# Routing with the dot-product row in PSUM, all four look-up scalings on ScalarE, and more rows fetched

## The chip, the cores and the metric

The kernel runs on one core of a Trainium2 chip (trn2). The metric is the device time of one execution, in microseconds (us); the time given is the median of several runs. Times inside an execution come from one profiled execution of the same program.

## The reference, cut to what matters

The reference is two transformer blocks over 512 tokens of 1024 features. Only the end of the second block is touched: a mixture of 16384 single-row experts (PEER), chosen by product keys.

```python
def peer_ffn(u, w_q, sub_keys, u_tab, v_tab):        # u: 512 tokens x 1024
    q = (xt @ w_q).reshape(T, H, 2, PEER_DKEY // 2)   # 8 heads, 2 halves
    s = jnp.einsum('thcd,hcnd->thcn', q, sub_keys)    # 128 keys a half
    top_s, top_i = lax.top_k(s, K)                    # K = 16
    cand = top_s[:, :, 0, :, None] + top_s[:, :, 1, None, :]
    best_s, best_j = lax.top_k(cand.reshape(T, H, K * K), K)
    expert = ...                                      # i * 128 + j of the 16 best pairs
    g = jax.nn.softmax(best_s, axis=-1)
    act = gelu(einsum('cd,chkd->chk', xc, u_tab[expert]))
    return einsum('chk,chkd->cd', g * act, v_tab[expert])
```

The last step of all is an RMS norm of the residual plus this sum.

## The kernel before, in words

The kernel computes the experts in two ways. For the first 128 tokens it **fetches** the chosen rows: 128 steps gather one row of `u_tab` for each token (GpSimd, indirect DMA, 512 KB, `grow`, 7 buffers) and take the dot product with the token's row `xr` on VectorE (L1252), and 128 more gather rows of `v_tab` and add them up (L1263). Each of the two runs has six steps of lag, so there are 268 steps in all (`self.left`, L1210). For the other 384 tokens it computes **all** experts densely: 128 blocks, each of 24 matmuls over 384 columns (`mm<-ushi,whi` and its kin, L136 to L138), a Gelu (L119) and later three products with the rows of `v_tab` for each of three token blocks (L1567). The gate of each expert and token is made by **look-up matrices**: for four tokens at a time `onehots` (L1420) compares a row of numbers (`iota`, in the PSUM tile `tables`) with the chosen indices, which gives J and I, and multiplies I by the token's weights; four matmuls J x I (L1449) then write a group `pg` into PSUM, and ScalarE copies it to `stg` (L1450), from where it goes to memory (`Gd`). There are 96 such groups, 32 for each of three token blocks.

In `onehots` the compare is one VectorE instruction (L1423). ScalarE then scales `NA` = 2 of the four I matrices (L1427) and VectorE the other two (L1428), with a copy `wp` of the weights in `tables`.

The order of the stage is set in `route`. First a loop over 16 score blocks (L1300 to L1325): a projection of 24 matmuls over 512 columns, four score matmuls into a PSUM tile `psc` (L1312), `topk` on VectorE; in its first eight rounds two transposes give a part of `xr` and of `gacc` (L1321 to L1325). The `tr` tile that they pass through has one buffer. Then, under `manual_schedule` for the PE, one dense block after another is issued (L1473 to L1483), and behind each so many steps of `routing()` as the block's credit pays for: `choose` (VectorE work that picks the experts of one token block) and `gates` (onehots three groups ahead, `AHEAD`, and the group's four matmuls). A block earns `UCOST` = 2.9 (4.04 before the fetching begins), a group costs `GCOST` = 0.7, a step of `choose` 1 to 6.6. The PE executes in exactly this order. The other engines' orders are laid out by the framework's planner, which takes, for each engine, the earliest issued instruction among those that it holds for ready; each engine executes its queue in order.

After each block `fetch_steps(RATE * (256 - e))` (L1483) adds to a credit `left / units` fetch steps. By the costs in the source 61 blocks are issued in this loop and 45 of the 268 fetch steps.

PSUM has eight banks: two for `mm`, four for `psc` and `pg` together (one tag), one for `tr`, one for `tables`. At the end of `route` its six banks are given back, and `combine` takes them as six accumulators `acc`, which first receive transposes of the residual (L1573). `combine` then runs the remaining blocks, the products with `v_tab` and the remaining fetch steps.

Of the kernel before, what the change touches and what calls it, by code (L numbers as in the profile page):

```python
# [7 lines left out]
F32 = mybir.dt.float32  # L8
# [26 lines left out]
FLEAD = 4  # L35
LAST = 3
GCOST = 0.7
NA = 2
UCOST = 2.9
AHEAD = 3  # L40
RATE = 1.3


class Stream:
# [51 lines left out]
class Kernel:  # L96
# [1133 lines left out]
    def gathered(self, ep):  # L1230
# [15 lines left out]
        for k in range(P + lag):  # L1246
            if k < P:
                rows[k] = fetch(a["peer_ur_2"], k)
            if k >= lag:
                scr = ep.tile([P, D], BF16, name="gscr", tag="gscr", bufs=1)  # L1250
                with after():
                    nc.vector.scalar_tensor_tensor(scr, rows.pop(k - lag), 1.0, self.xr, op0=ALU.mult,  # L1252
                                                   op1=ALU.mult, accum_out=self.gact[:, k - lag:k - lag + 1])
            if k == P + lag - 1:
                self.act(self.gact, self.gact, AF.Gelu)
                nc.vector.tensor_tensor(self.gw, self.gw, self.gact, op=ALU.mult)
            yield
# [19 lines left out]
    def route(self, ep, rp, pp):  # L1277
        tc, nc, a = self.tc, self.nc, self.a
        sk = rp.tile([P, 16, P], F32, name="sk", tag="cand")
        nc.sync.dma_start(sk, a["peer_sk"])  # L1280

        iota_s = rp.tile([P, P], F32, name="iota", tag="tables")
        nc.gpsimd.iota(iota_s, pattern=[[1, P]], base=0, channel_multiplier=0, allow_small_or_imprecise_dtypes=True)
        tables = pp.tile([P, 3 * P + 16], F32, name="tables", tag="tables", bufs=1)
        iota, first = tables[:, :P], tables[:, 3 * P:]
        nc.vector.tensor_copy(iota, iota_s)
        tv = rp.tile([P, 4, 16, 16], F32, name="tv")
        tix = rp.tile([P, 4, 16, 16], U32, name="tix")
# [11 lines left out]
        for b in range(16):  # L1300
# [6 lines left out]
            qt = rp.tile([P, 2, S], F32, name="pq", tag="oh", bufs=AHEAD + 1)  # L1307
            q = qt[:, 0]
            nc.vector.tensor_tensor(q, ps, self.rstd, op=ALU.mult)
            pc = pp.tile([P, 4, P], F32, name="psc", tag="psc", bufs=4)  # L1310
            for tb in range(4):
                nc.tensor.matmul(pc[:, tb, :], q[:, tb * P:(tb + 1) * P], sk[:, b, :], start=True, stop=True)  # L1312
            for tb in range(4):
# [1 line left out]
            if b < 8:  # L1315
                t = qt[:, 1]
                nc.vector.scalar_tensor_tensor(t, self.xT[:, b, :], self.g["norm_ffn_2"][:, b:b + 1], self.rstd,
                                               op0=ALU.mult, op1=ALU.mult)
                self.split(self.us[0][:, b, :], self.us[1][:, b, :], t[:, P:])
                px = pp.tile([P, 2, P], F32, name="tr", tag="tr", bufs=1)  # L1320
                nc.tensor.transpose(px[:, 0], t[:, :P], self.ident)  # L1321
                nc.tensor.transpose(px[:, 1], self.xT[:, b, :P], self.ident)
                bs = slice(b * P, (b + 1) * P)
                nc.scalar.activation(self.xr[:, bs], px[:, 0], AF.Copy)
                nc.scalar.activation(self.gacc[:, bs], px[:, 1], AF.Copy)  # L1325


# [21 lines left out]
        def choose(tb):  # L1349
# [62 lines left out]
                nc.tensor.transpose(pt[:, c, :], ijw[:, c].rearrange("p h k -> p (h k)"), self.ident)  # L1412
            t = rp.tile([P, 3, P], F32, name="ijwT", tag="ijwT", bufs=2)
            nc.vector.tensor_copy(t, pt[:, :3])
            wp = tables[:, (1 + tb % 2) * P:(2 + tb % 2) * P]
            nc.vector.tensor_copy(wp, t[:, 2])
            T[tb] = t, wp
            yield 1.0

        def onehots(t, wp, x0):  # L1420

            oh = rp.tile([P, 2, 4, P], F32, name="oh", tag="oh", bufs=AHEAD + 1)
            nc.vector.tensor_tensor(oh, iota[:, None, None, :].to_broadcast([P, 2, 4, P]),  # L1423
                                    t[:, 0:2, x0:x0 + 4, None].to_broadcast([P, 2, 4, P]), op=ALU.is_equal)
            I, J = oh[:, 0], oh[:, 1]
            for c in range(NA):
                nc.scalar.activation(I[:, c], I[:, c], AF.Copy, scale=t[:, 2, x0 + c:x0 + c + 1])  # L1427
            self.last_gate = nc.vector.tensor_tensor(I[:, NA:], I[:, NA:], wp[:, x0 + NA:x0 + 4, None]  # L1428
                                                     .to_broadcast([P, 4 - NA, P]), op=ALU.mult)
            return J, I  # L1430

        def gates(tb):

            t, wp = T.pop(tb)
            oh = {}
            for x in range(0, 4 * AHEAD, 4):
                oh[x] = onehots(t, wp, x)
                yield 1.2
            for part in range(4):
                self.write(len(self.pieces) - P // PIECE)  # L1440
                stg = self.cp.tile([P, P, 32], F32, name="stg", tag="xlo" if part % 2 else "xhi")
                for k in range(8):
                    x = 32 * part + 4 * k
                    if x + 4 * AHEAD < P:
                        oh[x + 4 * AHEAD] = onehots(t, wp, x + 4 * AHEAD)
                    J, I = oh.pop(x)
                    pg = pp.tile([P, 4, P], F32, name="pg", tag="psc", bufs=4)
                    for c in range(4):
                        nc.tensor.matmul(pg[:, c, :], J[:, c], I[:, c], start=True, stop=True)  # L1449
                    nc.scalar.activation(stg[:, :, 4 * k:4 * k + 4], pg.rearrange("p c i -> p i c"), AF.Copy)  # L1450
                    yield GCOST
# [45 lines left out]
    def combine(self, ep, e):  # L1497
        tc, nc, a = self.tc, self.nc, self.a
        with tc.tile_pool(name="pv", bufs=1) as vp, tc.tile_pool(name="pvp", bufs=1, space=PSUM) as pp:
            self.ws.all_vector = True  # L1500
            ng = vp.tile([P, D], F32, name="ng")
            nc.gpsimd.dma_start(ng, a["norm_final_2"].to_broadcast([P, D]))
            vh = self.cp.tile([P, 4, D], F32R, name="vh", tag="xhi")
# [206 lines left out]
```

## Time and profile before

| | us |
|---|---|
| median of 3 runs | 2456.24 (2454.66 to 2459.8) |
| profiled execution, its own time | 2457.38 |
| span of the profiled execution, first to last instruction | 2455.7 |
| score stage of the routing (16 projections) | about 1173 to 1276 |
| choosing for the first two token blocks | 1276 to 1357 |
| gates, first two token blocks, with choosing between | 1357 to 1555 |
| gates, third token block | 1555 to 1628 |
| change to `combine` | 1628 to 1672 |
| `combine` | 1672 to 2448 |

In the views, PE is TensorE's matmuls, PEld its weight loads, DVE is VectorE, ACT ScalarE, POOL GpSimd. A form such as `oh<-tables,ijwT` names the tile written and the tiles read. Matmuls are pipelined and their recorded durations overlap, so the pace of a run of matmuls is read from starts, not from durations. Each matmul record of L1449 is one of two that a 128x128 product in fp32 leaves, so a group has eight.

### The profile page before, as it was taken

To read this page: it belongs to the slowest core of one execution; us is meant where nothing else is said; L and a number is where in the kernel's file an instruction comes from. 1 tells how busy PE (TensorE), PEld (TensorE's weight loads), DVE (VectorE), ACT (ScalarE), POOL (GpSimd) and SP (SyncE) were. 2 spreads that over 40 slices of the span, in tenths; PEclk is the share of its full clock that TensorE was granted. 3 is DMA by queue.
4 is the path that set the end of the run, shared out by engine and by line. 5 is a ranking of instruction groups with operands and counts; after the bars stand their busy time and mean duration, and the time that the engine had idled before them with its cause. 6 is when DMAs were issued, how large, how long until landed. Compare 5 with 4: busy or idle time off the path is not lost.

```text
span 2455.7 us, 32561 instructions
## 1 busy us (share of the span) xinstructions
PE 2388.6 (97%) x11857; PEld 2019.8 (82%) x11857; DVE 1765.5 (72%) x3088; ACT 1085.1 (44%) x1847; POOL 981.5 (40%) x564
## 2 busy tenths in 40 slices
PE   8999999999999999999999999989999999999998
PEld 6776788888776767887789999989888888888887
DVE  7986777721567564365999998967887678777884
ACT  5565332322466575434323656653333333333333
POOL 5332444444542313542336556533343234434430
PEclk9999999999999999999999999999999999999999
DMA  4111233333322202231236687889999889998981
GB/s 139 61 60 44 95 94 96 99 89 96 114 93 73 86 27 69 95 107 65 78 97 221 217 293 265 296 325 354 322 344 343 287 289 343 340 322 310 339 305 69
DMA packets 178673, 451.96 MB, mean 184 GB/s; under 512 B 16480, under 2 KB 83200, under 8 KB 175312
## 3 DMA queue, kind: packets, MB, share of 16 engines
q1 hardware_dynamic: 129616, 299.07, 36.1%
q0 software_dynamic: 37232, 135.07, 15.1%
q10 hardware_dynamic: 11664, 15.74, 1.8%
q8 instruction: 93, 1.52, 0.3%
q14 instruction: 68, 0.56, 0.1%
HBM read 409.98 MB, written 39.85 MB: 183 GB/s over the span
## 4 chain that ended last, share of the span: by engine, by line
PE 78%; DVE 15%; ACT 3%; issue 2%; POOL 1%; DMA 1%; ACTq 0%; SPq 0%; DVEq 0%; POOLq 0%
PE acc L1567 21%; PE mm L136 15%; PE mm L137 15%; PE mm L138 15%; PE pg L1449 3%; DVE cv L375 1%; DVE oh L1423 1%; PE av L1007 1%; PE tr L661 1%; DVE gscr L1252 1%; POOL wlo L74 1%; DMA vraw<-in_peer_v 1%; DVE xlo L172 1%; PE sc L637 1%; ACT whi L70 1%
## 5 line engine op out<-in xcount | busy, mean ns | idle before, releaser
L74 POOL TENSOR_TENSOR wlo<-wraw,whi 128x1024 fp32r<-128x1024 f32 (+1 forms) x250 | 602.5, 2412 | 825.0 <-ACT whi L70 761.9
L70 ACT ACTIVATE whi<-wraw 128x1024 fp32r<-128x1024 f32 (+1 forms) x319 | 334.4, 1049 | 608.5 <-PE mm L137 412.2
L136 PE MATMUL mm<-xhi,whi 128*128 128x512 f32 x952 | 383.5, 403 | 4.7 <-DVE gb L403 2.1
L138 PE MATMUL mm<-xhi,wlo 128*128 128x512 f32 x952 | 377.7, 397 | 1.3 <-POOL wlo L74 1.2
L137 PE MATMUL mm<-xlo,whi 128*128 128x512 f32 x952 | 377.4, 396 | 0.0
L136 PE MATMUL mm<-ushi,whi 128*128 128x384 f32 x1024 | 349.5, 341 | 9.5 <-ACT act L119 9.5
L138 PE MATMUL mm<-ushi,wlo 128*128 128x384 f32 x1024 | 346.0, 338 | 0.0
L137 PE MATMUL mm<-uslo,whi 128*128 128x384 f32 x1024 | 345.8, 338 | 0.0
L1567 PE MATMUL acc<-vh,galo 128*128 128x512 f32 x768 | 300.3, 391 | 0.0
L1567 PE MATMUL acc<-vl,gahi 128*128 128x512 f32 x768 | 300.2, 391 | 0.0
L1567 PE MATMUL acc<-vh,gahi 128*128 128x512 f32 x768 | 299.0, 389 | 0.0
L1238 POOL DMA_INDIRECT grow<-in_peer_v,gidx x128 | 184.7, 1443 | 269.8 <-DVE gacc L1263 254.5
L1238 POOL DMA_INDIRECT grow<-in_peer_ur,gidx x128 | 152.5, 1191 | 248.8 <-DVE gscr L1252 228.9
L136 PEld LDWEIGHTS mm<-xhi,whi 128*128 128x128 f32 x952 | 180.2, 189 | 46.9 <-issue 9.4
L137 PEld LDWEIGHTS mm<-xlo,whi 128*128 128x128 f32 x952 | 179.5, 189 | 40.8 <-issue 4.5
L138 PEld LDWEIGHTS mm<-xhi,wlo 128*128 128x128 f32 x952 | 179.9, 189 | 39.3 <-POOL wlo L74 1.9
L193 ACT ACTIVATE gahi<-gg 128x384 fp32r<-128x384 f32 x128 | 67.3, 526 | 319.4 <-PE acc L1567 245.2
L136 PEld LDWEIGHTS mm<-ushi,whi 128*128 128x128 f32 x1024 | 194.8, 190 | 12.6 <-ACT act L119 10.2
L137 PEld LDWEIGHTS mm<-uslo,whi 128*128 128x128 f32 x1024 | 194.5, 190 | 2.4
L138 PEld LDWEIGHTS mm<-ushi,wlo 128*128 128x128 f32 x1024 | 194.3, 190 | 0.0
L72 DVE TENSOR_TENSOR wlo<-wraw,whi 128x1024 fp32r<-128x1024 f32 x69 | 85.8, 1244 | 137.8 <-ACT whi L70 137.7
L1252 DVE SCALAR_TENSOR_TENSOR gscr<-grow,xr 128x1024 bf16<-128x1024 f32 x128 | 176.3, 1377 | 0.5
(438 smaller groups left out, 4433.1 us busy)
## 6 DMA issues: line engine op xcount, KB each, us to landing
wraw<-in_peer_u SPq DMA_DIRECT2D x128, 512.0 KB, 4.5
vraw<-in_peer_v SPq DMA_DIRECT2D x128, 512.0 KB, 6.9
Gd<-stg SPq DMA_DIRECT2D x24, 1024.0 KB, 8.9
rgat<-Gd SPq DMA_DIRECT2D x32, 768.0 KB, 9.7
wraw<-in_w_up SPq DMA_DIRECT2D x44, 512.0 KB, 3.5
Ad<-act ACTq DMA_DIRECT2D x64, 192.0 KB, 4.0
ract<-Ad SPq DMA_DIRECT2D x64, 192.0 KB, 7.5
wraw<-in_w_in SPq DMA_DIRECT2D x20, 512.0 KB, 3.5
```

The source lines that it names most:

```text
L70: self.nc.scalar.activation(hi[:, :w], raw[:, :w], AF.Copy)
L72: self.nc.vector.tensor_tensor(lo[:, :w], raw[:, :w], hi[:, :w].bitcast(F32), op=ALU.subtract)
L74: self.last_split = self.nc.gpsimd.tensor_tensor(lo[:, :w], raw[:, :w], hi[:, :w].bitcast(F32), op=ALU.subtract)
L136: mm(ps, w[0], x[0], start=start, stop=False)
L137: mm(ps, w[0], x[1], start=False, stop=False)
L138: mm(ps, w[1], x[0], start=False, stop=stop)
L172: nc.vector.scalar_tensor_tensor(lo[:, db, :n], xb, g[:, db:db + 1], hi[:, db, :n].bitcast(F32), op0=ALU.mult, op1=ALU.subtract)
L193: self.nc.scalar.activation(hi, src, AF.Copy)
L1238: nc.gpsimd.indirect_dma_start(out=t, out_offset=None, in_=tab.rearrange("a b d -> (a b) d"), in_offset=bass.IndirectOffsetOnAxis(ap=self. ...
L1252: nc.vector.scalar_tensor_tensor(scr, rows.pop(k - lag), 1.0, self.xr, op0=ALU.mult, op1=ALU.mult, accum_out=self.gact[:, k - lag:k - lag ...
L1449: nc.tensor.matmul(pg[:, c, :], J[:, c], I[:, c], start=True, stop=True)
L1567: mm(acc[tb][h], x[:, ts], v[:, i % 4, ds], start=False, stop=(i == P - 1 and x is lo), skip_group_check=True)
```

## The change

- `xps`, a PSUM tile of 128x1024 fp32 (two banks), takes in the first eight score rounds a copy of what `xr` takes, by one VectorE copy of 128x128 a round. While the routing runs, the dot products of the fetched rows read `xps` instead of `xr`; from `combine` on they read `xr` again.
- `onehots` loses VectorE's multiplication: ScalarE scales all four I matrices. `wp` and its copy are gone, and `tables` shrinks within its bank.
- `psc` and `pg` have two buffers together instead of four, which frees the two banks for `xps`.
- `RATE` goes from 1.3 to 1.05: by the source 55 instead of 45 fetch steps are issued in the routing loop. The number of blocks, the groups behind each and the costs stay as they are.

```diff
-NA = 2
-RATE = 1.3
+RATE = 1.05
...
+                x = self.xr if self.xps is None else self.xps
...
-                    nc.vector.scalar_tensor_tensor(scr, rows.pop(k - lag), 1.0, self.xr, op0=ALU.mult,
+                    nc.vector.scalar_tensor_tensor(scr, rows.pop(k - lag), 1.0, x, op0=ALU.mult,
...
+        self.xps = pp.tile([P, D], F32, name="xps")
...
-        tables = pp.tile([P, 3 * P + 16], F32, name="tables", tag="tables", bufs=1)
-        iota, first = tables[:, :P], tables[:, 3 * P:]
+        tables = pp.tile([P, P + 16], F32, name="tables", tag="tables", bufs=1)
+        iota, first = tables[:, :P], tables[:, P:]
...
-            pc = pp.tile([P, 4, P], F32, name="psc", tag="psc", bufs=4)
+            pc = pp.tile([P, 4, P], F32, name="psc", tag="psc", bufs=2)
...
                 nc.scalar.activation(self.xr[:, bs], px[:, 0], AF.Copy)
+                nc.vector.tensor_copy(self.xps[:, bs], px[:, 0])
...
-            wp = tables[:, (1 + tb % 2) * P:(2 + tb % 2) * P]
-            nc.vector.tensor_copy(wp, t[:, 2])
-            T[tb] = t, wp
+            T[tb] = t
...
-            nc.vector.tensor_tensor(oh, iota[:, None, None, :].to_broadcast([P, 2, 4, P]),
+            self.last_gate = nc.vector.tensor_tensor(oh, iota[:, None, None, :].to_broadcast([P, 2, 4, P]),
                                     t[:, 0:2, x0:x0 + 4, None].to_broadcast([P, 2, 4, P]), op=ALU.is_equal)
             I, J = oh[:, 0], oh[:, 1]
-            for c in range(NA):
+            for c in range(4):
                 nc.scalar.activation(I[:, c], I[:, c], AF.Copy, scale=t[:, 2, x0 + c:x0 + c + 1])
-            self.last_gate = nc.vector.tensor_tensor(I[:, NA:], I[:, NA:], wp[:, x0 + NA:x0 + 4, None]
-                                                     .to_broadcast([P, 4 - NA, P]), op=ALU.mult)
...
-                    pg = pp.tile([P, 4, P], F32, name="pg", tag="psc", bufs=4)
+                    pg = pp.tile([P, 4, P], F32, name="pg", tag="psc", bufs=2)
...
+            self.xps = None
```

## Rows read from the trace of the kernel before

**Rows 1.** The page, part 1: busy time, share of the span, instructions.

```profile
PE 2388.6 (97%) x11857; PEld 2019.8 (82%) x11857; DVE 1765.5 (72%) x3088; ACT 1085.1 (44%) x1847; POOL 981.5 (40%) x564
```

**Rows 2.** Busy time by stretch; columns in the first line.

```profile
core 0: us, PE busy (x) PEld busy (x) DVE busy (x) ACT busy (x) POOL busy (x), PEclk, DMA share, GB/s
1173.00:1276.00 103.00, 102.48 (x515) 83.42 (x514) 99.82 (x533) 22.15 (x40) 35.70 (x15) 1.00 0.25 79
1276.00:1357.40 81.40, 74.43 (x412) 73.34 (x410) 80.47 (x288) 30.76 (x43) 45.53 (x24) 0.96 0.58 192
1357.40:1555.00 197.60, 194.92 (x1283) 194.28 (x1284) 186.58 (x277) 123.05 (x255) 115.43 (x63) 0.99 0.77 270
1555.00:1628.40 73.40, 73.40 (x526) 73.23 (x524) 68.52 (x93) 53.20 (x124) 35.01 (x22) 1.00 0.81 290
1672.00:2448.00 776.00, 776.00 (x3748) 683.99 (x3747) 593.65 (x748) 276.76 (x391) 281.98 (x205) 1.00 0.86 306
```

**Rows 3.** PE's waits from 1165 to 1680: total us, times, longest us.

```profile
PE mm L136 <- ACT act L119: 9.5, 2, 6.3
PE tr L1412 <- DVE ijw L1345: 2.1, 1, 2.1
PE tr L1412 <- DVE tmp L1344: 1.6, 1, 1.6
PE pg L1449 <- ACT oh L1427: 1.4, 2, 1.0
PE pg L1449 <- DVE oh L1428: 1.3, 1, 1.3
PE acc L1573 <- ACT stg L1450: 1.0, 1, 1.0
```

**Rows 4.** Groups of instructions, 1354 to 1630: count | busy us, mean ns | idle before, releaser.

```profile
L1423 DVE TENSOR_TENSOR oh<-tables,ijwT 128x1024 f32<-128x1024 f32 x96 | 116.9, 1218 | 8.4 <-ACT whi L70 3.9 <-PE pg L1449 3.7
...
L1252 DVE SCALAR_TENSOR_TENSOR gscr<-grow,xr 128x1024 bf16<-128x1024 f32 x42 | 71.3, 1698 | 0.2
...
L1427 ACT ACTIVATE oh<-oh,ijwT 128x128 f32<-128x128 f32 x192 | 68.0, 396 | 70.7 <-DVE oh L1423 68.9
...
L1238 POOL DMA_INDIRECT grow<-in_peer_ur,gidx x41 | 45.6, 1111 | 50.1 <-DVE gscr L1252 37.3 <-PE mm L138 7.1 <-issue 2.0
L1428 DVE TENSOR_TENSOR oh<-oh,tables 128x256 f32<-128x256 f32 x96 | 40.1, 417 | 2.5
```

**Rows 5.** The same view in `combine`, 1700 to 1945, where POOL runs no arithmetic.

```profile
L1252 DVE SCALAR_TENSOR_TENSOR gscr<-grow,xr 128x1024 bf16<-128x1024 f32 x72 | 87.9, 1220 | 0.2
```

**Rows 6.** Timeline of ACT in a block with four groups: start, us, instruction, wait before.

```profile
1604.25 1.06 ACT L70 ACTIVATE whi<-wraw 128x1024 fp32r<-128x1024 f32 x1 [1.04 <-issue]
1605.21 0.47 ACT L119 ACTIVATE act<-mm 128x384 f32<-128x384 f32 x1
1605.58 0.39 ACT L1427 ACTIVATE oh<-oh,ijwT 128x128 f32<-128x128 f32 x1
...
1606.39 0.58 ACT L1450 ACTIVATE stg<-pg 128x512 f32<-128x512 f32 x1
1606.87 0.68 ACT L1427 ACTIVATE oh<-oh,ijwT 128x128 f32<-128x128 f32 x2
1607.46 1.07 ACT L1450 ACTIVATE stg<-pg 128x512 f32<-128x512 f32 x2
```

**Rows 7.** Timeline of PE, runs of groups of L1449 (eight records a group).

```profile
1539.58 2.84 PE L1449 MATMUL pg<-oh 128*128 128x128 f32 x24
...
1604.17 3.73 PE L1449 MATMUL pg<-oh 128*128 128x128 f32 x32
1611.91 3.73 PE L1449 MATMUL pg<-oh 128*128 128x128 f32 x32
```

**Rows 8.** Timeline of ACT, the first copy behind the run of three groups of rows 7.

```profile
1540.98 0.59 ACT L1450 ACTIVATE stg<-pg 128x512 f32<-128x512 f32 x1
```

**Rows 9.** Timeline of DVE: a copy of 128x128 into PSUM.

```profile
1423.11 0.28 DVE L1401 COPY tr<-ixf 128x128 f32<-128x128 f32 x1
```

More of the change, by code (lines that the diff above doesn't have):

```diff
@@ L1414, in choose, with onehots @@
             nc.vector.tensor_copy(t, pt[:, :3])
-            wp = tables[:, (1 + tb % 2) * P:(2 + tb % 2) * P]
-            nc.vector.tensor_copy(wp, t[:, 2])
-            T[tb] = t, wp
+            T[tb] = t
             yield 1.0
-        def onehots(t, wp, x0):
+        def onehots(t, x0):
             oh = rp.tile([P, 2, 4, P], F32, name="oh", tag="oh", bufs=AHEAD + 1)
-            nc.vector.tensor_tensor(oh, iota[:, None, None, :].to_broadcast([P, 2, 4, P]),
+            self.last_gate = nc.vector.tensor_tensor(oh, iota[:, None, None, :].to_broadcast([P, 2, 4, P]),
                                     t[:, 0:2, x0:x0 + 4, None].to_broadcast([P, 2, 4, P]), op=ALU.is_equal)
             I, J = oh[:, 0], oh[:, 1]
-            for c in range(NA):
+            for c in range(4):
                 nc.scalar.activation(I[:, c], I[:, c], AF.Copy, scale=t[:, 2, x0 + c:x0 + c + 1])
-            self.last_gate = nc.vector.tensor_tensor(I[:, NA:], I[:, NA:], wp[:, x0 + NA:x0 + 4, None]
-                                                     .to_broadcast([P, 4 - NA, P]), op=ALU.mult)
             return J, I
         def gates(tb):
-            t, wp = T.pop(tb)
+            t = T.pop(tb)
             oh = {}
             for x in range(0, 4 * AHEAD, 4):
-                oh[x] = onehots(t, wp, x)
+                oh[x] = onehots(t, x)
                 yield 1.2
@@ L1444, in gates @@
                     if x + 4 * AHEAD < P:
-                        oh[x + 4 * AHEAD] = onehots(t, wp, x + 4 * AHEAD)
+                        oh[x + 4 * AHEAD] = onehots(t, x + 4 * AHEAD)
                     J, I = oh.pop(x)
-                    pg = pp.tile([P, 4, P], F32, name="pg", tag="psc", bufs=4)
+                    pg = pp.tile([P, 4, P], F32, name="pg", tag="psc", bufs=2)
                     for c in range(4):
```

## The prediction

> **What bounds the kernel now.** I read the busy times first: TensorE is at 97% of the span [rows 1]. An average can hide a stage with another limit, so the stretches come next [rows 2]. In `combine` the PE is busy in all of 776 us, and no wait of it is recorded there: nothing that the change moves into or out of `combine` can shorten it. In the routing, 1276 to 1628, the reader sees two engines near their limit at once: the PE at 74.43 of 81.4, 194.92 of 197.6 and 73.4 of 73.4 us, VectorE at 80.47, 186.58 and 68.52. VectorE looks like the bound, but it is so only where the PE waits, and the waits of the PE [rows 3] are short: 3.7 us at L1412 and 3.2 of the 9.5 us at L136, both before the first gate, while VectorE chooses the experts of the second token block; 1.4 + 1.3 = 2.7 us behind onehots; then, at the change to `combine`, 1.0 us for the last copy and 6.3 us for a Gelu. That is 17.2 us in all. The PE's order and its work stay as they are, so this sum is the ceiling of any gain, and only the 2.7 us hang on what the change relieves.
>
> **VectorE's relief.** The removed multiplications are 96 x 0.417 = 40.1 us [rows 4]. The dot products took 1.698 us in the routing and 1.220 us in `combine`, where POOL runs no arithmetic [rows 4, 5]. The compare of onehots has as many elements and one operand in PSUM, and took 1.218 us under the same POOL [rows 4]. So I take 1.22 us for a dot product with `xps`, 42 x 0.478 = 20.1 us less; the bounds are 1.70 and 1.22. [...] Ten more fetch steps add 10 x 1.3 = 13 us. VectorE's load from 1357 to 1628 falls from 255 to 255 - 40 - 20 + 13 = 208 of 271 us. What that is worth is the wait behind it: 2.7 us, bounds 0 and 2.7. The 6.9 us before the first gate stay: in that stretch there is no dot product and no onehot yet.
>
> **The copies into `xps`.** Eight copies of 128x128, 0.28 us each [rows 9], go to VectorE in the score stage, 2.2 us. VectorE has 3.2 us idle there and the PE 0.5 [rows 2], so the PE paces the stage and VectorE's gaps take the copies; I count 0. If that cover is gone they lengthen the later wait at L1412 by up to 2.2 us. The copy is queued on VectorE ahead of `topk`, and `tr` (one buffer) is not free before it is done; the next transposes come a round later.
>
> **Ten fetch steps moved.** Each is a descriptor instruction on POOL, a 512 KB transfer and a dot product. POOL: 10 x 1.1 us [rows 4] beside 150 of 271 us busy [rows 2]; queued behind it is the weights' low half (`wlo`), of which two blocks are in stock. The DMA engines are at 0.77 to 0.81 [rows 2]; 5 MB in 271 us are 19 GB/s beside 270 to 290. Cost 0, bounds 0 and some 3 us at the change to `combine`, where the transfers collide with those of `vraw`. `acc` now takes over the banks of `xps` and so waits for the last dot product of the routing; one or two of them may still run then, 0 to 2.4 us [rows 5]. In `combine` ten steps less gain nothing, for the PE was never idle there.
>
> **ScalarE and the two buffers.** This is the term that counts. Two scalings in a row start 0.59 us before the next copy (1606.87 to 1607.46, [rows 6]). Two more for each of 96 groups are 96 x 0.59 = 57 us. Between 1555 and 1628 ScalarE goes from 53.2 to 53.2 + 32 x 0.59 = 72 of 73.4 us: it becomes as full as the PE. In 1357 to 1555 it goes from 123 to 161 of 197.6. [...]
>
> Now the buffers. A group takes the PE 3.73 - 2.84 = 0.89 us, and a block with four groups comes every 7.74 us [rows 7]. With four buffers a run of four groups waits for nobody. With two, the third group waits for the copy of the first, the fourth for that of the second. Take the run at 1604.17 [rows 7]: the third group would start at 1604.17 + 1.78 = 1605.95, but ScalarE first works through the split of weights, the Gelu and two scalings, and ends the first copy at 1606.39 + 0.58 = 1606.97 [rows 6]: 1.02 us late. The third group then ends at 1607.86, the second copy at about 1608.0: another 0.15. So 1.2 us for a run of four with ScalarE's queue as it was. If two more scalings stand ahead of each copy, the first copy comes 1.6 us late and the second another 0.75: 2.35 us. If the copy stands ahead of the scalings, as in the run of three at 1539.58 (third group due at 1541.36, first copy done at 1540.98 + 0.59 = 1541.57, [rows 7, 8]), it is 0.2 us. For a run of four there is a floor all the same: ScalarE's own sequence, 5.8 us in rows 6 (0.96 + 0.37 + 0.2 for the queued store, and four times 0.59 + 0.48), becomes 8.2 us in a block of 7.74: 0.45 us.
>
> By the source's credits 9 blocks have four groups or five, 12 have three. Low: 9 x 0.45 + 12 x 0 = 4. High: 9 x 2.35 + 12 x 1.6 = 40. I take 1.2 for fours, in the middle, since VectorE, now early, lets ScalarE do some scalings while the dense block runs but also lets the planner put others ahead of a copy; and 0.3 for threes, near the row of 1539, because ScalarE has slack there: 9 x 1.2 + 12 x 0.3 = 14.4.
>
> **Sum.** 14.4 - 2.7 = +11.7 us on the profiled execution's 2457.4: 2469.1. That execution stands 1.1 us above the median of the runs, so 2468.
>
> **Rivals.** (a) *Copies first.* The planner lays the copies ahead of the scalings nearly everywhere, and VectorE's waits vanish: 9 x 0.45 + 12 x 0.2 - 2.7 = +3.8, so 2460: not slower by what can be told. For it: the orders at 1539 [rows 8]; against it: the run at 1604 [rows 6], and in a block's issue order the scalings of the group three ahead stand before the copy. (b) *Scalings first everywhere*: 40 us and no gain, 2457.4 - 1.1 + 37 to 40, some 2495. It decides once 1.2 us of scalings stand between the Gelu and the first copy of a block. (c) *Faster at the change to `combine`*, one mechanism: the 6.3 us Gelu there [rows 3] is queued behind other work of ScalarE. If the new order puts it ahead, 6.3 us go, and with 2.7 us of onehot waits and the floor of 3 to 4 us the kernel takes 2456.2 - 6.3 - 2.7 + 3.5 = 2451 or a little less. Against it: nothing of the change touches that place but the banks and the fetches, and these rather add. (d) *The PSUM operand does not speed the dot products*: then VectorE stands at 228 of 271 us, still below its old 255, and the time is as in the forecast.
>
> **How the numbers follow.** Forecast (2462 to 2476, d included) 0.46; b and what leads to it, above 2476, 0.16; a, 2452 to 2461, 0.27; c, below 2451, 0.11. A measurement of this kernel can tell about 0.2%, 4.9 us, from no change, so faster than 2451.3 counts as faster and slower than 2461.1 as slower: 0.11, 0.27, 0.62. The range leaves out the far part of b and of c: 2450 to 2487.
>
> **What would show it.** In the profile of the changed kernel: no L1428; L1252 at about 1.22 us in the routing; VectorE near 77% from 1357 on; four scalings a group and ScalarE above 90% in the last token block's gates; waits of the PE's `pg` matmuls for ScalarE (`stg`), most at the third and fourth group of a run, some 14 us together; blocks with four groups 8.2 to 10 us apart instead of 7.74; `combine` at its 776 us. I am wrong if the PE's waits for `stg` are below 5 us, if the pace of these blocks stays at 7.74, or if the score stage, with two buffers now, stretches.

## The result, and the profile after

| | before | after |
|---|---|---|
| median (7 runs each) | 2456.24 us | 2469.07 us |
| lowest and highest | 2452.47 to 2459.8 | 2464.66 to 2472.25 |
| profiled execution, span | 2457.38, 2455.7 | 2469.26, 2467.5 |

The ratio of after to before is 1.0052, with a 95% interval of 1.0039 to 1.0065: 9.6 to 16.0 us slower. The forecast was 2468. The total agrees, but the terms of the sum do not, and most of what follows is about that.

Part 1 of the page of the changed kernel, to lay beside [rows 1]:

```profile
PE 2390.6 (97%) x11857; PEld 2018.4 (82%) x11857; DVE 1711.0 (69%) x2997; ACT 1143.4 (46%) x2039; POOL 970.6 (39%) x564
```

TensorE has the same instructions and the same share. VectorE is 54 us lighter and ScalarE 58 us heavier; nothing in this line tells that the kernel became slower. The stretches do, in the view that answers to [rows 2]; each of the first four stretches begins and ends at nearly the same work as there, and the last two are cut at the first product in `acc`, at 1684.90 (columns as in [rows 2]):

```profile
1173.00:1276.00 103.00, 102.56 (x522) 84.82 (x522) 100.84 (x549) 25.21 (x41) 36.25 (x16) 1.00 0.25 82
1276.00:1359.80 83.80, 72.44 (x402) 71.32 (x401) 82.83 (x278) 30.18 (x46) 46.60 (x25) 0.95 0.58 195
1359.80:1558.00 198.20, 195.64 (x1266) 193.60 (x1267) 152.35 (x229) 157.56 (x374) 114.47 (x69) 0.99 0.79 283
1558.00:1647.60 89.60, 80.19 (x542) 76.81 (x540) 57.06 (x65) 73.82 (x192) 38.52 (x25) 1.00 0.75 266
1647.60:1684.90 37.30, 34.99 (x218) 34.62 (x218) 17.17 (x19) 14.99 (x22) 1.83 (x3) 1.00 1.02 378
1684.90:2460.00 775.10, 775.10 (x3742) 682.88 (x3741) 582.89 (x728) 276.88 (x390) 268.70 (x196) 1.00 0.85 301
```

The gates of the third token block take 89.6 us where they took 73.4, and the PE, busy in all of it before, is idle for 9.4 us. The score stage (103 us) and `combine` have kept their length (from the first product in `acc` to the last 775.7 us before and 775.6 after). There are two smaller differences: the stretch before the first gate is 2.4 us longer, and the change to `combine` is shorter. The PE's waits from 1160 to 1700 (us, times, longest) answer to [rows 3]:

```profile
PE pg L1447 <- ACT stg L1448: 10.3, 11, 1.5
PE mm L135 <- ACT act L118: 6.8, 2, 5.5
PE tr L1414 <- DVE tmp L1346: 2.9, 1, 2.9
PE tr L1414 <- DVE ijw L1347: 2.1, 1, 2.1
PE acc L1572 <- ACT stg L1448: 1.0, 1, 1.0
PE tr L1414 <- DVE ijw L1380: 0.9, 1, 0.9
```

The waits for onehots are gone, a new wait of the `pg` matmuls for the copies to `stg` has come, and the Gelu waits have changed places: 5.5 us now stand before the first gate (3.2 in [rows 3]) and 1.3 us at the change to `combine` (6.3 there).

For all kernels below I cut the routing at three marks. The **way** runs from the first score matmul to the first matmul after the PE's Gelu wait ahead of the first gate; the **gates** from there to the first transpose into `acc`; the **change** from there to the first product in `acc`. These lengths are differences of start times in the timeline of the PE of one profiled execution each; a ratio is taken to runs of the kernel before on the same chip, so that rows are better compared by ratios than by medians:

| kernel | way | gates | change | median us | ratio to before |
|---|---|---|---|---|---|
| before | 183.2 | 272.0 | 43.6 | 2456.24 | |
| after | 186.0 | 288.8 | 36.2 | 2469.07 | 1.0052 [1.0039, 1.0065] |
| e1_two_buffers | 183.2 | 293.6 | 40.3 | 2476.66 | 1.0087 [1.0073, 1.0100] |
| e2_four_scalings | 183.6 | 269.8 | 43.4 | 2454.02 | 0.9997 [0.9988, 1.0006] |
| e3_rate | 186.7 | 279.2 | 42.4 | 2463.14 | 1.0036 [1.0023, 1.0050] |
| e4_copies_first | 186.0 | 277.4 | 42.4 | 2462.57 | 1.0030 [1.0018, 1.0041] |
| e8_old_rate | 182.4 | 289.2 | 38.2 | 2467.90 | 1.0058 [1.0045, 1.0072] |
| e9_psum_row_only | 182.0 | 285.8 | 40.9 | 2464.93 | 1.0042 [1.0028, 1.0056] |
| e10_gelu_first | 183.6 | 269.9 | 42.7 | 2453.66 | 0.9996 [0.9987, 1.0005] |
| e11_no_fetch | 183.6 | 269.8 | 34.7 | 2445.16 | 0.9957 [0.9943, 0.9971] |
| e12_both | 183.6 | 269.9 | 34.6 | 2446.15 | 0.9965 [0.9953, 0.9977] |
| e13_after_no_fetch | 186.0 | 288.8 | 34.6 | 2466.46 | 1.0043 [1.0029, 1.0057] |

From before to after the three stretches change by +2.8, +16.8 and -7.4: +12.2 us (the spans differ by 11.8; the median by 12.8).

### The profile page after: what moved, and what is told of

Same layout as the page of the kernel before. It is cut to its first block, busy times and chain, and to the rows that moved or that the text cites. A ratio compares the mean times of both kernels' runs of the same rounds, so it can differ in the third digit from the quotient of the medians.

```text
span 2467.5 us, 32759 instructions
## 1 busy us (share of the span) xinstructions
PE 2390.6 (97%) x11857; PEld 2018.4 (82%) x11857; DVE 1711.0 (69%) x2997; ACT 1143.4 (46%) x2039; POOL 970.6 (39%) x564
## 3 DMA queue, kind: packets, MB, share of 16 engines
q1 hardware_dynamic: 129616, 299.07, 36.2%
## 4 chain that ended last, share of the span: by engine, by line
PE 79%; DVE 12%; ACT 5%; issue 2%; DMA 1%; POOL 1%; DVEq 0%; SPq 0%; POOLq 0%; ACTq 0%
PE acc L1566 21%; PE mm L135 16%; PE mm L136 16%; PE mm L137 15%; PE pg L1447 2%; DVE cv L374 1%; ACT oh L1427 1%; PE av L1006 1%; ACT whi L69 1%; PE tr L660 1%; POOL wlo L73 1%; DVE xlo L171 1%; PE sc L636 1%; PE psc L1313 1%; PE sc L637 0%
## 5 line engine op out<-in xcount | busy, mean ns | idle before, releaser
L1237 POOL DMA_INDIRECT grow<-in_peer_ur,gidx x128 | 146.8, 1147 | 219.0 <-DVE gscr L1252 195.9
L136 PEld LDWEIGHTS mm<-xlo,whi 128*128 128x128 f32 x952 | 179.6, 189 | 40.9 <-issue 4.5
L1566 PEld LDWEIGHTS acc<-vh,galo 128*128 128x128 f32 x768 | 144.1, 188 | 30.1
```

The costliest lines, as they stand in the source:

```text
L136: mm(ps, w[0], x[1], start=False, stop=False)
L1237: nc.gpsimd.indirect_dma_start(out=t, out_offset=None, in_=tab.rearrange("a b d -> (a b) d"), in_offset=bass.IndirectOffsetOnAxis(ap=self. ...
L1566: mm(acc[tb][h], x[:, ts], v[:, i % 4, ds], start=False, stop=(i == P - 1 and x is lo), skip_group_check=True)
```

## The experiments

**Each part alone.** Three kernels take one part of the change each onto the kernel before.

Two buffers for `psc` and `pg`, nothing else:

```diff
-            pc = pp.tile([P, 4, P], F32, name="psc", tag="psc", bufs=4)
+            pc = pp.tile([P, 4, P], F32, name="psc", tag="psc", bufs=2)
...
-                    pg = pp.tile([P, 4, P], F32, name="pg", tag="psc", bufs=4)
+                    pg = pp.tile([P, 4, P], F32, name="pg", tag="psc", bufs=2)
```

> The kernel before with one edit: the PSUM tiles of the score and gate groups have two buffers instead of four. Between the first gate block and the transposes at the change to combine the kernel before took 272.0 us, the changed one 288.8. If the loss comes from two buffers with copies queued behind scalings (buffer theory), the PE waits for the copies here too, about 0.6 to 1.5 us in each of some 20 runs of three or four groups: the stretch grows by 8 to 15 us and the time is 2464 to 2470. If it comes from ScalarE's 57 us of added load (load theory), nothing changes here: 272 us and 2456. VectorE's load is that of before, so the change to combine (43.8 us from the transposes to the first product, 36.4 in the changed kernel) stays near 44 if VectorE's lateness sets it.

Measured: 22 us slower by the medians, the gates 21.6 us longer and the change to `combine` 3.3 us shorter; the way is 183.2 as before, so the score stage does not miss the two buffers. The cost is larger than I expected and larger than that of the whole change. The PE waits for the copies, by up to 4.2 us at once:

```profile
PE pg L1449 <- ACT stg L1450: 15.2, 15, 4.2
```

Four scalings on ScalarE, with four buffers:

```diff
-NA = 2
+NA = 4
...
-            self.last_gate = nc.vector.tensor_tensor(I[:, NA:], I[:, NA:], wp[:, x0 + NA:x0 + 4, None]
-                                                     .to_broadcast([P, 4 - NA, P]), op=ALU.mult)
```

> The kernel before with one edit: ScalarE scales all four look-up matrices, with four buffers as before. Buffer theory: the PE hardly waits for copies; ScalarE needs 8.2 us in a block of 7.74, so the gates' stretch is 270 to 276 us. Load theory: 285 to 289 us as in the changed kernel. VectorE loses 40 us; if its lateness sets the change to combine, that shrinks from 43.8 to about 37 us. So 2447 to 2454 by the buffer theory with the lateness, 2456 to 2460 without the lateness, 2464 or more by the load theory.

Measured: no difference that can be told. The gates are 2.2 us shorter. The onehot waits are gone (no `pg` matmul has a wait in the list): the two blocks that they lengthened, at 1370 and 1482 in the kernel before, come out 0.9 and 2.9 us shorter, 3.8 together, more than the 2.7 us of [rows 3]. What the scalings cost shows in the pace: the last four runs of four groups come every 8.1 to 8.2 us instead of 7.74 [rows 7], 1.6 us together; the runs ahead of them keep their pace. Timeline of the PE in e11_no_fetch, which has the same gates:

```profile
1600.36 4.12 PE L1446 MATMUL pg<-oh 128*128 128x128 f32 x32
1608.52 4.11 PE L1446 MATMUL pg<-oh 128*128 128x128 f32 x32
```

That is ScalarE's own sequence, worked out as 8.2 us in the prediction. The change to `combine` stays at 43.4: neither VectorE's relief nor the moved scalings shorten it.

`RATE` alone:

```diff
-RATE = 1.3
+RATE = 1.05
```

> The kernel before with one edit: the rate constant 1.05, so ten more fetch steps in the routing. VectorE has 255 us of work in 271 there and gets ten dot products of 1.3 to 1.8 us more: 268 to 273, so it is full. If VectorE then paces the gates, their stretch grows by 2 to 10 us and the change to combine gets no shorter: 2457 to 2468. If the extra fetches alone were what shortened the change to combine in the changed kernel, 43.8 falls to about 37 us and the time is 2449 to 2455.

Measured: 8.8 us slower: way +3.5, gates +7.2, change -1.2. With dot products of 1.698 us on a VectorE that is busy in 255 of 271 us (kernel before, [rows 2, 4]), ten more fetch steps are not free.

**The order of ScalarE's queue.** The changed kernel, with a group's matmuls and copy issued ahead of the onehots of the group three ahead:

```diff
-                    if x + 4 * AHEAD < P:
-                        oh[x + 4 * AHEAD] = onehots(t, x + 4 * AHEAD)
                     J, I = oh.pop(x)
...
                     nc.scalar.activation(stg[:, :, 4 * k:4 * k + 4], pg.rearrange("p c i -> p i c"), AF.Copy)
+                    if x + 4 * AHEAD < P:
+                        oh[x + 4 * AHEAD] = onehots(t, x + 4 * AHEAD)
```

> The changed kernel with one edit: the matmuls and the copy of a group are issued before the onehots of the group three ahead, so that a copy goes before those scalings on ScalarE. Buffer theory: the wait of 1.0 us at the fourth group goes and 0.4 us at the third stays; blocks with four groups come every 8.2 to 8.5 us instead of 9.4, the gates' stretch is 276 to 281 us instead of 288.8, the time 2456 to 2462. Load theory: 9.4 us and 2469 stay.

Measured: 2462.57, 0.6 us above what was expected and 6.5 us below the changed kernel (the intervals of the two ratios just touch), and the gates 11.4 us shorter (277.4). In the last token block a run of four now comes every 8.28 us, and the fourth group waits 0.2 us instead of 1.0:

```profile
1602.43 2.90 PE L1445 MATMUL pg<-oh 128*128 128x128 f32 x24
1605.53 1.16 PE L1445 MATMUL pg<-oh 128*128 128x128 f32 x8 [0.19 <-ACT stg L1446]
1610.71 2.90 PE L1445 MATMUL pg<-oh 128*128 128x128 f32 x24
```

So the time that the two buffers cost in the changed kernel is set by what stands ahead of the copies. The rest of the 11.4 us does not arrive, for the change to `combine` takes 42.4 us here and not 36.2.

**Parts on top of one another.** The changed kernel with `RATE` = 1.3:

```diff
-RATE = 1.05
+RATE = 1.3
```

> The changed kernel with RATE back at 1.3 (45 instead of 55 fetch steps in the routing). Theory: the 2.8 us longer way from the first score matmul to the first gate come from two dot products that the higher number of steps puts into VectorE's choosing; so the way falls back to 183 to 184 us and, the gates stretch staying near 288 us (their copies wait in ScalarE's queue, not for VectorE), the time is 2464 to 2467. Rival: the eight copies into xps lengthen that way; then it stays at 186 us and the time at 2469. Second rival: the ten dot products also lengthen the gates; then the gates fall to 281 us or less and the time to 2461 or less.

The way falls to 182.4 and the gates stay (289.2). The first half of the theory holds: the longer way belongs to `RATE`, not to the eight copies into `xps`. The time does not follow: 2467.9 is 0.9 us above what I expected and cannot be told from the changed kernel. In this kernel the ten steps cost the way 3.6 us in the profile, and nothing that the runs can show.

The two buffers and the row in PSUM, with two scalings still on VectorE and `RATE` = 1.3, against the kernel before:

```diff
+                x = self.xr if self.xps is None else self.xps
...
-                    nc.vector.scalar_tensor_tensor(scr, rows.pop(k - lag), 1.0, self.xr, op0=ALU.mult,
+                    nc.vector.scalar_tensor_tensor(scr, rows.pop(k - lag), 1.0, x, op0=ALU.mult,
...
+        self.xps = pp.tile([P, D], F32, name="xps")
...
+                nc.vector.tensor_copy(self.xps[:, bs], px[:, 0])
...
-                    pg = pp.tile([P, 4, P], F32, name="pg", tag="psc", bufs=4)
+                    pg = pp.tile([P, 4, P], F32, name="pg", tag="psc", bufs=2)
```

> The kernel before with two buffers for psc and pg and the dot-product row in PSUM, but two of the four scalings still on VectorE and RATE 1.3: what e1_two_buffers becomes when the dot products take 1.21 instead of 1.70 us. Theory: e1 lost 20 us since a copy came late when VectorE, nearly full, was late with the scalings that stand ahead of it on ScalarE; 20 us less of VectorE's work take back about half: gates stretch 280 to 286 us, time 2463 to 2469. Rival: only the order of ScalarE's queue counts, then it stays as e1, gates 292 us or more, time 2474 or more. If it lies below e8_old_rate by over 3 us, the move of the scalings to ScalarE is what costs; if above by over 3 us, the move gains.

Against e1, the faster dot products take 7.8 us out of the gates and 11 us out of the time (10.3 above before instead of 21.4; each ratio times 2455). The rival (only the queue order counts) falls. Block by block, all of the 7.8 us lie in the first two token blocks, in their runs of three and the one run of four, while VectorE also chooses; the runs behind that take the same time in e1 and e9. Moving the other two scalings to ScalarE (e9 to e8) adds 3.4 us to the gates and 3.0 to the time; the two intervals overlap, so I call this term small and do not sign it.

**The change to `combine`.** It became 7.4 us shorter, and no part of the change aims at it. In the kernel before, the Gelu that the PE waits for stands in ScalarE's queue behind three copies `vh`, which wait for the transfers of `vraw`. Timeline of ACT, kernel before:

```profile
1648.39 1.06 ACT L1549 ACTIVATE vh<-vraw 128x1024 fp32r<-128x1024 f32 x1 [7.80 <-DMA vraw<-in_peer_v]
...
1652.33 1.06 ACT L1549 ACTIVATE vh<-vraw 128x1024 fp32r<-128x1024 f32 x1 [0.39 <-DMA vraw<-in_peer_v]
1653.29 0.47 ACT L119 ACTIVATE act<-mm 128x384 f32<-128x384 f32 x1
```

This reads like a matter of queue order. So e10 holds the copies behind a Gelu, on the kernel of e2:

```diff
             for i in range(FLEAD):
                 fresh(i)
+            early = self.cur_users[-3]
...
-                nc.scalar.activation(vh[:, i % 4, :], r, AF.Copy)
+                with tc.issue_after(early.ins) if i < 4 else ExitStack():
+                    nc.scalar.activation(vh[:, i % 4, :], r, AF.Copy)
```

> The kernel of e2_four_scalings (four buffers, four scalings on ScalarE, xr in SBUF) with the first four copies vh of combine held behind the Gelu of the second fresh dense block, so that no Gelu stands behind a copy that waits for the transfer of vraw. Theory: the 6.3 us wait of TensorE at the change to combine, and the stretch of 0.32 us matmuls at the low granted clock that follows it, are caused by that queue order alone: the change to combine takes 34 to 37 us instead of 43.5 and the time is 2444 to 2449, below both kernels. Rival: the transfers of vraw themselves are late for the first products; then the wait only moves to the first acc products and the time stays at 2452 to 2455.

Measured: 42.7 us and no gain. In the kernel of e2, on which e10 is built, the change has two waits for a Gelu, 2.41 us behind the copies `vh` and 2.70 us behind a split `whi`. In e10 the copies went where I put them, and a wait stayed: the Gelu now stands behind the split `whi` of the next weights, which waits for its own transfer. ACT's waits and the PE's timeline in e10_gelu_first:

```profile
ACT whi L70 <- DMA wraw<-in_peer_u: 16.0, 2, 10.8
```

```profile
1653.11 0.69 PE L136 MATMUL mm<-ushi,whi 128*128 128x384 f32 x1 [5.27 <-ACT act L119]
```

My theory fell. Whatever comes first in the queue, some transfer is late. The DMA share says the same, 1.02 and 1.03 from 1632 on (kernel before):

```profile
1632.00:1640.00 8.00, 8.00 (x58) 8.00 (x57) 0.93 (x2) 0.85 (x1) 2.48 (x3) 1.00 1.02 370
1640.00:1650.00 10.00, 7.56 (x44) 7.24 (x42) 1.75 (x2) 1.64 (x3) 0.00 (x0) 1.00 1.02 419
1650.00:1660.00 10.00, 6.19 (x21) 6.19 (x22) 6.65 (x6) 5.71 (x7) 0.00 (x0) 0.66 1.03 347
```

And just ahead of `vraw` (issued at 1635.08) POOL issues row after row, 512 KB each, for VectorE frees the buffers as soon as the last onehots are done: behind their last multiplication, at 1622.06, five dot products follow one another from 1622.40 to 1629.37. Six in the kernel before between 1626 and 1635, timeline of POOL:

```profile
1626.70 0.95 POOL L1238 DMA_INDIRECT grow<-in_peer_ur,gidx  x1 [0.30 <-issue]
...
1634.15 0.94 POOL L1238 DMA_INDIRECT grow<-in_peer_ur,gidx  x1 [0.30 <-issue]
```

So e11 takes fetch steps away from this place, again on the kernel of e2; e12 does so on e10. The steps are made up for later, in `combine`; no row fetch is issued between 1575 and 1665 in e11, and up to 1665 there are 40 instead of the 51 of e2, eleven fewer:

```diff
-                self.fetch_steps(RATE * (256 - e))
+                if e <= 54:
+                    self.fetch_steps(RATE * (256 - e))
...
-                self.fetch_steps(units[0] - 6)
+                if units[0] < 2 * P - e0 - 6:
+                    self.fetch_steps(units[0] - 6)
```

> The kernel of e2_four_scalings without fetch steps in the last seven blocks of the routing loop and in the first of combine (they are made up for later in combine). In e10 the wait at the change to combine stayed and its releaser changed from the copies vh to the splits whi that waited for the transfer of weights, with the DMA engines above 1.0 of their time from 1632 to 1660 in the kernel before. Theory: the change to combine is bound by transfers, and the rush of nine row fetches of 512 KB just ahead of the transfers of vraw, freed when the last gates are done, makes it so; without some six of them (3 MB, 8 us at the 390 GB/s of that stretch) the change takes 36 to 39 us instead of 43.4 and the time is 2446 to 2450. Rival: only the queue order counts or the fetches are not what fills the engines: change 42 to 44 us, 2453 to 2455.

> The same on top of e10_gelu_first: fewer row fetches and the copies vh behind a Gelu. Theory: with the transfers thinned out the queue order of ScalarE is what is left of the wait: change to combine 33 to 37 us, time 2443 to 2448. Rival: the weights' transfers still queue behind those of vraw, and the order is worth nothing here either: within 2 us of e11_no_fetch.

Measured: the change takes 34.7 us, the PE has no Gelu wait there at all, and the time is 2445.16, below both kernels (ratio to before 0.9957); both are a little better than expected. e12 is the same within 1 us: with the transfers thinned out, the order of ScalarE's queue is worth nothing, and without that (e10) it was worth nothing either. The cause is the crowd of row fetches ahead of `vraw`. (The edit takes ten dot products out of that time too; but in e2 and e10 ScalarE's queue waits there for transfers, `vraw` and `wraw`, not for VectorE.) The same windows in e11_no_fetch:

```profile
1632.00:1640.00 8.00, 8.00 (x50) 8.00 (x49) 1.23 (x1) 1.44 (x2) 0.00 (x0) 1.00 1.01 418
1640.00:1650.00 10.00, 10.00 (x59) 9.97 (x58) 7.18 (x6) 6.79 (x8) 0.00 (x0) 1.00 1.05 362
1650.00:1660.00 10.00, 10.00 (x60) 10.00 (x59) 6.05 (x8) 5.25 (x8) 0.00 (x0) 1.00 0.99 330
```

The DMA engines are as full as before; but no row fetch is among what they carry, and the PE is busy throughout.

Last, the same edit on the changed kernel:

> The changed kernel without the fetch steps at the end of the routing loop and at the start of combine (the edit of e11_no_fetch). Theory: in the changed kernel the longer gates leave the transfers more time, which already gave back 5 to 7 us of the change to combine; so here the edit finds less to take: change to combine 34.6 us as in e11, gates 284 to 289 us, time 2464 to 2467, 2 to 4 us below the changed kernel where e11 gained 9 on its own base. The distance to e11_no_fetch, 19 to 22 us, is then the cost of the change without the part given back. Rival: the changed kernel's shorter change to combine is worth nothing in particular, and the edit gains some 8 us here too: 2460 to 2462.

Measured: change 34.6, gates 288.8, 2466.46: the edit finds 2.6 us here where it found 8.9 on the kernel of e2 (2454.02 to 2445.16); the 2.6 us are not clear of noise, for the intervals of the two ratios overlap. Against e11, which has the same change to `combine`, the changed kernel costs 21.3 us (21.1 by the ratios). That is its price where nothing is given back. Four scalings are in both kernels; e2 shows that on their own they cost nothing that can be told.

A second profile of each kernel shows how firm the lengths are. The kernel before gave 183.2, 272.0 and 43.4 again. The changed kernel gave 186.0 and 288.8 again, but 38.8 for the change to `combine`, with a Gelu wait of 2.56 us where the first profile has 1.31. The expectations were these:

> The kernel before once more, for a second profile. If the lengths of the stretches belong to the program, the change to combine takes 43.6 us within 1 us, the wait behind the Gelu 6.25 us and the gates 272 us; in after_again the change to combine came out 2.6 us longer than in the profile of the changed kernel, so 41 to 46 us would say that this stretch varies by that much.

> The changed kernel once more, for a second profile of the same program. Theory: the lengths of its stretches are fixed by its queue orders: way to the first gate 186.0, gates 288.8, change to combine 36.3, each within 1 us. Rival: the change to combine varies from execution to execution (36 to 44 us), so its 7.4 us are not the kernel's own.

So the way and the gates belong to the program; the change to `combine` in the changed kernel moves by some 2.6 us from execution to execution, and the 7.4 us given back are 5 to 7.

## Why the prediction was right in its total and wrong in its terms

**The runs of four were mis-sized.** This was the term that counts, with 9 x 1.2 = 10.8 us. The mechanism is as told: the third group waits for the copy of the first, the fourth for that of the second. Timeline of the PE in the changed kernel, to lay beside [rows 7]:

```profile
1609.01 3.21 PE L1447 MATMUL pg<-oh 128*128 128x128 f32 x24
1613.23 1.16 PE L1447 MATMUL pg<-oh 128*128 128x128 f32 x8 [1.01 <-ACT stg L1448]
1618.41 3.21 PE L1447 MATMUL pg<-oh 128*128 128x128 f32 x24
```

The blocks are 9.40 us apart instead of 7.74: 1.66 each, made of 0.37 at the third group (a run of three takes 3.21 instead of 2.84, and the view shows no wait for that), 1.01 at the fourth, and 0.28 until the dense block is under way. Seven runs cost 1.64 to 1.68, one at 1448.79 1.83, the run of five 2.40: 15.9 us where 10.8 was forecast.

The 1.2 us itself was right for the queue from which it was worked out, with two scalings ahead of a copy. In e9, which has that queue and two buffers, the blocks are 9.07 and 8.83 us apart, 1.33 and 1.09 more than 7.74, and its nine runs cost 10.3 us together. Timeline of the PE in e9, starts of three runs of four:

```profile
1601.78 1.95 PE L1451 MATMUL pg<-oh 128*128 128x128 f32 x16
...
1610.85 3.21 PE L1451 MATMUL pg<-oh 128*128 128x128 f32 x24
...
1619.68 1.95 PE L1451 MATMUL pg<-oh 128*128 128x128 f32 x16
```

So the part that was sized wrong is what two more scalings for each group add to a run with two buffers. The prediction took 1.2 as the middle between 0.45 and 2.35, which leaves nothing for them; they came to 0.6 us a run. The runs of three, which cost 6.2 us together in e9 and 3.8 in the changed kernel, give 2.4 us of that back; so e8 stands only 3.4 us above e9 in the gates.

I also had it the wrong way round where the time is spent. I expected the first copy to be late, by 1.02, and the second by 0.15. ACT's timeline of that block shows the first copy right behind the Gelu, ahead of all scalings, as rival (a) wanted, and every later copy behind four of them:

```profile
1609.08 1.06 ACT L69 ACTIVATE whi<-wraw 128x1024 fp32r<-128x1024 f32 x1 [0.81 <-issue]
1610.04 0.47 ACT L118 ACTIVATE act<-mm 128x384 f32<-128x384 f32 x1
1610.41 0.59 ACT L1448 ACTIVATE stg<-pg 128x512 f32<-128x512 f32 x1
...
1611.41 1.28 ACT L1427 ACTIVATE oh<-oh,ijwT 128x128 f32<-128x128 f32 x4 [0.41 <-DVE oh L1423]
1612.60 0.57 ACT L1448 ACTIVATE stg<-pg 128x512 f32<-128x512 f32 x1
1613.08 1.26 ACT L1427 ACTIVATE oh<-oh,ijwT 128x128 f32<-128x128 f32 x4
1614.25 0.58 ACT L1448 ACTIVATE stg<-pg 128x512 f32<-128x512 f32 x1
```

Second copy: 1612.60 + 0.57 = 1613.17, and the fourth group starts at 1613.23. Scalings and copies take turns, and 0.41 us of the gap is ScalarE's wait for a compare. VectorE starts the first of three compares at 1610.15 and ends it at about 1611.4, in DVE's timeline:

```profile
1610.15 3.48 DVE L1423 TENSOR_TENSOR oh<-tables,ijwT 128x1024 f32<-128x1024 f32 x3 [3.21 <-ACT whi L69]
```

The view names `whi`, done at 1609.08 + 1.06 = 1610.14. By the program the compare needs the `oh` buffer that a group of matmuls gives back, and the first group of the run ends at the same moment, 1609.01 + 1.16 = 1610.17; which of the two it was the times do not tell, and I take the buffer. Then the pace is set by a ring of waits through three engines: group, compare, scalings, copy, group. I had put it at the sum of ScalarE's work. ScalarE is idle for 0.81 + 0.41 of the 9.4 us here, and for longer where a block has fewer groups; so it stands at 82% in the last token block's gates (73.82 of 89.6) and not above 90%.

**The floor and rival (a).** The floor of 8.2 us is right for a queue without that ring: 8.16 in e11, 8.28 in e4. (a) has the right mechanism and nearly the right price where the copies do come first: +3.8 was worked out for the gates, and e4 has +5.4 there. It was not what the planner did with the changed kernel: one copy of four came first.

**The runs of three** were 12 x 0.3 = 3.6. The traces have eleven; eight cost 0.39 each, the others 0.49, 0.13 and 0.06, together 3.8. Held.

**VectorE's relief** held in its parts and was somewhat larger in its price. The dot product takes 1.210 us with `xps`, compares 1.218, VectorE's load from the first gate to the end of the gates is 152.35 + 57.06 = 209 us where 208 was worked out, and the onehot waits are gone; as in e2, the two blocks with these waits give back 3.8 us, not 2.7. Groups of instructions, 1354 to 1645, to lay beside [rows 4]:

```profile
L1427 ACT ACTIVATE oh<-oh,ijwT 128x128 f32<-128x128 f32 x384 | 123.0, 392 | 39.9 <-DVE oh L1423 39.4
L1423 DVE TENSOR_TENSOR oh<-tables,ijwT 128x1024 f32<-128x1024 f32 x96 | 114.4, 1218 | 71.9 <-ACT whi L69 56.6 <-PE pg L1447 11.8 <-ACT act L118 2.6
...
L1252 DVE SCALAR_TENSOR_TENSOR gscr<-grow,xps 128x1024 bf16<-128x1024 f32 x47 | 56.9, 1210 | 0.1
```

VectorE now waits 72 us ahead of its compares (8 in [rows 4]), and ScalarE 39 us for them ahead of its scalings (69 there). Rival (d) is out. But I undervalued this relief: e1 and e9 show that without it the two buffers cost 22 us and with it 10. I had counted it only for the wait that it removes, and not for the copies that would come late if VectorE were late.

**Zero for the stretch before the first gate was wrong.** The prediction said that no dot product is in that stretch. The changed kernel has two there, in the midst of VectorE's choosing. Timeline of DVE, changed kernel:

```profile
1342.06 1.16 DVE L1252 SCALAR_TENSOR_TENSOR gscr<-grow,xps 128x1024 bf16<-128x1024 f32 x1
...
1343.15 0.28 DVE L1380 TENSOR_TENSOR ijw<-ijw,wsm 128x128 f32<-128x128 f32 x1
1343.36 1.20 DVE L1252 SCALAR_TENSOR_TENSOR gscr<-grow,xps 128x1024 bf16<-128x1024 f32 x1
```

In the kernel before, the first one starts at 1357.40. A smaller `RATE` issues the steps earlier, not only more of them; I had looked at where the extra steps lie in number and not at where the first one comes. It costs 2.8 us in the profile (3.6 between e8 and the changed kernel). The zero for the eight copies into `xps` held: without the higher number of steps the way is 182.0 and 182.4 (e9, e8). Behind the longer Gelu wait, 5.53 instead of 3.29 us, the first block of the gates takes 6.72 us instead of 5.84: the mean granted clock there is 0.60 (1359.83 to 1366.55) where it was 0.71 (1357.40 to 1363.24). These 0.9 us are in no term of the sum either.

**Zero for the change to `combine`, bounds 0 and +3, was wrong in sign.** It is 5 to 7 us shorter. Rival (c) saw that the 6.3 us Gelu wait could go, but put it down to the order of ScalarE's queue; e10 shows that the order is worth nothing. The wait is the crowd of transfers (e11). That the changed kernel gives it back since its longer gates let the row fetches drain before `vraw` is argued, not shown: all kernels with gates of 285 us or more have a change of 36 to 41 us, those with 280 or less 42 to 44, e11 to e13 apart; and in the changed kernel one row fetch lies in the 5.3 us ahead of `vraw`, where four did. Shown is that fewer fetches shorten it (e11), and that the same edit takes less from the changed kernel: 34.6 us in e13, 1.6 or 4.2 us below its two profiles, where e11 lies 8.7 below e2.

So +19.7 for the runs instead of +14.4, -3.8 for the onehot waits instead of -2.7, +0.9 for the slow start of the gates instead of 0, +2.8 before the gates instead of 0, and -7.4 behind them instead of 0: 12.2 where 11.7 was forecast. The step that failed in size is the run of four; the two terms at zero failed outright. Those two add up to -4.6 and nearly cancel the 5.3 that the main term lacked. The total was close partly by luck; with the second profile's change to `combine` the same sum is 14.8.

Two smaller readings of the prediction are off. The waits of [rows 3] that it adds up to 17.2 us come to 16.9. And this sum is no ceiling of any gain: the last section shows that a stall of 6.25 us cost 8.9.

## What to carry to other kernels

Two buffers between two engines cost least here where the consumer's copy comes next in its queue (the fourth group waits 0.19 us in e4, 1.01 us in the changed kernel): look at what else stands there between two copies (here four scalings of 0.29 us each), and at whether the engine that feeds those is itself late. With the same two buffers e1, e9 and the changed kernel lost 22, 10 and 13 us; they differ in the work around the copy.

A stall that names an instruction in a queue may be a stall of transfers (here another order left the change to `combine` at 42.7 us, fewer fetches made it 34.7). If putting another instruction first only changes the name of the releaser, look at what the DMA engines carry just before, and move the transfers that nobody waits for yet.

A stage that becomes slower can give some of it back at the next stage, where transfers had been the bound (here 5 to 7 us of 16.8). A part is then best priced against a kernel in which that stall is gone: 21.3 us here, not 12.8.

## What the runs showed of the hardware that was not expected

**The dot product of two SBUF operands does not have one length.** Its mean of 1.698 us [rows 4] hides a median of 1.224 and a tail up to 3.279 (shortest, median and longest in ns, kernel before to 1630):

```profile
L1252 DVE SCALAR_TENSOR_TENSOR gscr<-grow,xr x42: 1168/1224/3279, 1357.4 to 1628.1; 128x1024 bf16<-128x1024 f32 x42
```

With `xps` all lie between 1.200 and 1.220 from 1358 on. Of the 42, 16 take longer than 1.25 us, and each of these starts while POOL's `wlo` is running. Two timelines of the kernel before, POOL and DVE:

```profile
1567.61 2.39 POOL L74 TENSOR_TENSOR wlo<-wraw,whi 128x1024 fp32r<-128x1024 f32 x1 [1.27 <-ACT whi L70]
```

```profile
1569.16 1.92 DVE L1252 SCALAR_TENSOR_TENSOR gscr<-grow,xr 128x1024 bf16<-128x1024 f32 x1
```

POOL is done at 1570.00; from there 1.22 us would end at 1571.22, and the dot product ends at 1571.08. All 16 end 1.08 to 1.09 us after the `wlo`, within 0.14 us of a dot product that stands still until POOL is done. In the four cases in which the dot product starts first, it keeps its 1.21 to 1.22 us, and the `wlo` takes 2.68 to 3.06 us instead of 2.4. With `xps` neither is seen: 25 of the 47 dot products from 1358 on start while `wlo` is running, and none of these takes more than 1.220 us; the longest `wlo` up to 1641 takes 2.465 us. Why dot products grow longer beside a `wlo` with `xr` and not with `xps`, the traces do not show. The gain of the row in PSUM hangs on how many dot products meet a `wlo`; in the last token block of the kernel before it was 3 of 13.

**The stall at the change to `combine` costs more than its 6.25 us.** At its end the granted clock is low for a while: 0.50 from 1653 to 1659, with a mean of 0.66 from 1650 to 1660 and 1.00 again from 1660 to 1670; from 1654.30 to 1659.10 the matmuls start 0.32 us apart, and 0.17 from 1659.30 on. PE's timeline, kernel before:

```profile
1653.81 0.69 PE L136 MATMUL mm<-ushi,whi 128*128 128x384 f32 x1 [6.25 <-ACT act L119]
...
1654.62 0.52 PE L138 MATMUL mm<-ushi,wlo 128*128 128x384 f32 x1
1654.94 0.52 PE L136 MATMUL mm<-ushi,whi 128*128 128x384 f32 x1
...
1659.47 0.34 PE L136 MATMUL mm<-ushi,whi 128*128 128x384 f32 x1
```

43.6 - 34.7 = 8.9 us went with the wait in e11: 6.25 of waiting and some 2.6 that go with the matmuls 0.32 us apart (an estimate, the rest of the 8.9). The 1.31 us wait of the changed kernel, which ends at 1668.10, has no such stretch behind it: the granted clock there is 1.00 from 1665 to 1675.
